# The second feed-forward layer of a Trainium2 decoder step without a plain pair: seven products for its first pair of hidden tiles too, three of them on plain blocks ahead

## The chip, the core and the metric

The kernel runs on one core of a Trainium2 chip. The metric is the device time of one execution in microseconds (us). Five engines work side by side, each through its own queue in order: TensorE multiplies matrices (PE in the rows, PEld for its weight loads), VectorE (DVE) and ScalarE (ACT) work elementwise, GpSimd (POOL) adds squares, and SyncE (SP) issues the DMAs that bring weights from HBM. Semaphores order them.

## The reference

One inference step of a decoder trunk of two layers over 544 tokens (512 of a prompt, 32 of eight samples), model width 1024. Each layer has a half feed-forward, a token mixer (a gMLP in the first layer, attention in the second), a second half feed-forward and a gated embedding. What matters here is the gMLP's end and the feed-forward behind it:

```
def rmsnorm(x, g):
    y = xf * lax.rsqrt(jnp.mean(xf * xf, axis=-1, keepdims=True) + EPS)
    return (y * g.astype(jnp.float32)).astype(x.dtype)
def swiglu(x, w1, w3, w2):
    return (jax.nn.silu(x @ w1) * (x @ w3)) @ w2
...
        h = h + 0.5 * swiglu(rmsnorm(h, ffn1_norm[i]), ffn1_w1[i], ffn1_w3[i], ffn1_w2[i])
        ...
            mix, v_rows = gmlp_mix(xn, gmlp_w_in[i], gmlp_v_norm[i], gmlp_w_s[i], gmlp_b_s[i], gmlp_w_out[i])
        h = h + mix
        h = h + 0.5 * swiglu(rmsnorm(h, ffn2_norm[i]), ffn2_w1[i], ffn2_w3[i], ffn2_w2[i])
```

`w1` and `w3` are 1024 x 2816, so there are 22 hidden tiles of 128, or 11 pairs.

## The kernel before

Everything is held transposed: the residual `h` lies in 8 chunks of 128 model rows by 544 tokens. For accuracy every float32 operand is split into a high and a low half (`_split`, `split_pair`, `prep`): ScalarE casts the high half, VectorE subtracts it for the low one, and each product is three matmuls (high by high, high by low, low by high).

**Two ways to multiply a pair of hidden tiles.** A plain pair is four calls of `tile_mm` (two hidden tiles, `w1` and `w3` of each): 8 blocks of 128 rows, three matmuls, two column groups (256 and 288 tokens), so 48 matmuls each. Every other pair goes by seven products (`ffn_steps.products`, names "1" to "7" as in `SEVEN`): weights are cut in four quarters a11, a12, a21, a22, tokens in two halves of 272, and chunks of `h` in pairs. Product 1 is a11 on the even chunks' first half, 2 is a12 on the odd chunks' first half, 3 is (a12 - sum 6) on the odd chunks' second half; 5, 6, 7 and 4 work on sums of chunk blocks, which `forms` makes for a pair of chunks: two scalings on ScalarE, three subtractions on VectorE, two splits. Weight sums are made by VectorE in `_sum`: 5 = a21 + a22, 6 = sum 5 - a11, 7 = a11 - a21. One product is 4 blocks x 3 x 2 = 24 matmuls of 272 columns; `evict` adds the seven sums up, and `gate` puts the norm's `rstd`, the silu and the product of the two branches behind it.

**What comes before the layer.** The gMLP ends with 8 tiles of `tile_mm(m)`. Behind each, VectorE adds the tile to `h[c]` and `on_chunk` (in `next_norm`) makes the next layer's operand chunk (`prep`), its square on ScalarE and the running sum of squares on GpSimd; `early` names chunks after which the forms of a pair are made at once. Forms 0 to 2 are made there; the fourth is made during the plain pair, by `more` in `ffn`. The row statistic `rstd` goes by four short matmuls on the summed squares (`rstd`), in the first plain tile.

**Order.** Weights stand in one list of pieces; `prepare` loads, sums and splits ahead of use by the three numbers of `self.ahead` (split, sums, load, in pieces). In the gMLP the order of each engine's instructions is made by the framework's scheduler, which works from its own estimate of times; in `ffn_steps` it is the order of the code, with `ffn_slots` listing products and second-matrix pieces. `PLAIN = (2, 1, 1, 1)` gives the plain pairs of the four feed-forwards.

Of the kernel before, what the change touches and what calls it, by code (L numbers as in the profile page):

```python
# [54 lines left out]
PLAIN = (2, 1, 1, 1)  # L55

SEVEN = "1562734"

# [36 lines left out]
class Builder:  # L95
# [37 lines left out]
    def set_stream(self):  # L133
        self.chain, self.pending, self.bg, self.pages = None, [], [], {}
        self.aps, self.raws = [], {}
        self.pieces, self.sums, self.split = [], {}, {}
# [12 lines left out]
    def seven(self, aps):  # L149
# [5 lines left out]
        for k, x, op, y in (("5", a21, "+", a22), ("6", (r, "5"), "-", a11), ("7", a11, "-", a21),  # L155
                            ("3", a12, "-", (r, "6"))):
            d[k] = dict(key=(r, k), sum=(x, op, y))
        for v in d.values():
            v.update(n=1024)
# [14 lines left out]

    def _sum(self):
        p = self.pieces[self.p_sum]
        self.p_sum += 1
        if p["sum"] is None:
            return
        a, op, b = p["sum"]  # L180
        get = lambda x: self._raw(x, 1024) if isinstance(x[1], int) else self.sums[x]
        a, b = get(a), get(b)
        t = self.flat(1024)
        self.nc.vector.tensor_tensor(t, a, b, ALU.add if op == "+" else ALU.subtract)  # L184
        self.sums[p["key"]] = t
# [184 lines left out]
    def ffn_slots(self, skip=1):  # L370
# [16 lines left out]
    def ffn_pieces(self, n):  # L387
# [4 lines left out]
        for kind, at, k, part in self.ffn_slots(PLAIN[n]):  # L392
            if kind == "g":
                if at not in d:
                    d[at] = self.seven([i["w13"][n, at - 1, x] for x in range(4)])
# [10 lines left out]
    def ffn(self, h, box, gcol, rstd, on_chunk, plain=1):  # L406
# [33 lines left out]
        with self.tc.manual_schedule(engines={eng.PE, eng.Activation, eng.DVE, eng.Pool}):  # L440
            self.ffn_steps(h, xf, rstd, hid, todo, plain, on_chunk)
# [23 lines left out]
    def ffn_steps(self, h, xf, rstd, hid, todo, plain, on_chunk):  # L465
# [8 lines left out]
        def products(j, k, part):  # L474
            if k == "1" and j not in tiles:
                tiles[j] = {}
            t = tiles[j]
            if k in "152" and "ABC"["125".index(k)] not in t:
                if k == "2":
                    t["B"] = [self.pb()[:, :HT] for _ in range(2)]  # L480
                else:
                    t["A" if k == "1" else "C"] = self.ps()[:, :, :HT]
            out = t["A" if k in "1674" else "C" if k in "53" else "B"]
            dst = out if k == "2" else [out[:, w] for w in range(2)]
            hi, lo = self.take()
            for kp in range(NKP):
                xh, xl = xf[kp][k]
                for n, (a, b) in enumerate(((hi, xh), (hi, xl), (lo, xh))):
                    for w in range(2):
                        c = slice(512 * w + P * kp, 512 * w + P * kp + P)  # L490
                        nc.tensor.matmul(dst[w], a[:, c], b, start=k in "152" and kp == 0 and n == 0,  # L491
# [3 lines left out]
        def evict(j, k):  # L495
            t = tiles[j]
            if k in "156":
                t["r" + k] = q2(self.tmp())
                nc.scalar.copy(t["r" + k], t["C" if k == "5" else "A"])  # L499
                return  # L500
            if k == "2":
                t["g"] = self.big(), self.big()
            g = t["g"]
# [5 lines left out]
            elif k == "3":  # L509
                tt(g[0][:, :, HT:], t["C"], t["r6"], add)  # L510
                todo[0].extend(self.gate(hid, rstd, j, 0, g[0]))
            else:
# [57 lines left out]
    def gmlp(self, h, box, on_chunk):  # L570
# [94 lines left out]
        for c in range(NC_):  # L665
            p = self.tile_mm(m)
# [631 lines left out]
    def build(self):  # L1298
# [76 lines left out]
        on, nxt = self.next_norm(h, G_FFN2, early={1: 0, 3: 1, 5: 2})  # L1375
# [3 lines left out]
        self.ffn(h, box, G_FFN2, None, on)  # L1379
# [135 lines left out]
```

## Time and profile before

| what | value |
|---|---|
| time, median of 3 runs | 2065.02 us (2064.1 to 2067.02) |
| the profiled execution's own time | 2064.99 us |
| its span, first to last instruction | 2063.2 us |
| TensorE busy | 2043.9 us, 99%, 16432 matmuls |
| VectorE busy | 1507.6 us, 73% |
| ScalarE busy | 949.2 us, 46% |
| GpSimd busy | 186.9 us, 9% |
| granted TensorE clock, mean of the core | 1.000 |

The profile gives times from the span's start. A timeline row has the start, the time from its first instruction's start to its last one's end, engine, source line, operation, what it writes and reads, how many are merged, and in brackets how long the engine was idle before it and who ended that. A recorded duration holds a tail that the next instruction of the engine may overlap.

### The profile page before, as it was taken

How to read it: one execution, taken by the hardware profiler on the slowest of the kernel's cores; microseconds unless marked ns; L12 is line 12 of the kernel's file. 1: busy time of each engine (PE TensorE's matmuls, PEld its weight loads, DVE VectorE, ACT ScalarE, POOL GpSimd, SP SyncE). 2: the span in 40 equal slices, each digit the busy share in tenths (PEclk: the TensorE clock that was granted, in tenths of full speed). 3: DMA queues.
4: the chain of work that ended last, by engine and by line, in shares of the span. 5: the costliest groups of instructions: out<-in, count | busy, mean ns of one | idle time of the engine just before them, and what ended most of it. 6: DMA issues, size and time to landing. Idle time of an engine off the chain costs nothing.

```text
span 2063.2 us, 38844 instructions
## 1 busy us (share of the span) xinstructions
PE 2043.9 (99%) x16432; PEld 2012.0 (98%) x16432; DVE 1507.6 (73%) x1869; ACT 949.2 (46%) x1405; POOL 186.9 (9%) x238
## 2 busy tenths in 40 slices
PE   8999999999999999999999999999999999999999
PEld 8999999999999999999999999999987999999999
DVE  7877777556687777776688777776476888777774
ACT  7534344423554344454456343434364754344451
POOL 0000000410100000043060000001142200000020
PEclk9999999999999999999999999999999999999999
DMA  5233234312223232432374322324669322322431
GB/s 185 84 110 108 73 108 141 97 44 83 83 92 113 73 106 80 153 99 82 109 260 156 112 93 102 108 71 130 201 208 305 103 101 82 104 103 82 128 99 44
DMA packets 93807, 237.95 MB, mean 115 GB/s; under 512 B 9522, under 2 KB 27474, under 8 KB 93634
## 3 DMA queue, kind: packets, MB, share of 16 engines
q1 hardware_dynamic: 93490, 235.44, 34.4%
q8 instruction: 129, 2.11, 0.4%
q14 instruction: 44, 0.36, 0.1%
q10 hardware_dynamic: 144, 0.04, 0.0%
HBM read 218.95 MB, written 16.49 MB: 114 GB/s over the span
## 4 chain that ended last, share of the span: by engine, by line
PE 93%; DVE 3%; ACT 2%; issue 1%; DMA 1%; SPq 0%; POOL 0%; DVEq 0%; ACTq 0%
PE ps L491 33%; PE ps L241 16%; PE ps L247 16%; PE ps L245 16%; PE pb L491 5%; DVE big L199 1%; PE ps L1265 1%; PE ps L1269 1%; PE ps L1268 1%; ACT big L198 1%; PE ps L1222 0%; DVE big L184 0%; PE ps L829 0%; PE ps L830 0%; PE ps L831 0%
## 5 line engine op out<-in xcount | busy, mean ns | idle before, releaser
L491 PE MATMUL ps<-big,big 128*128 128x272 f32 x5616 | 727.7, 288 | 1.8 <-DVE big L508 1.3
L491 PEld LDWEIGHTS ps<-big,big 128*128 128x128 f32 x5616 | 714.2, 188 | 2.4 <-issue 1.6
L199 DVE TENSOR_TENSOR big<-big,big 128x1024 fp32r<-128x1024 f32 (+2 forms) x538 | 592.2, 1103 | 106.6 <-ACT big L198 106.0
L198 ACT CAST big<-big 128x1024 fp32r<-128x1024 f32 (+2 forms) x538 | 488.0, 932 | 267.8 <-DVE big L184 262.8
L241 PE MATMUL ps<-big,big 128*128 128x256 f32 (+1 forms) x2684 | 559.0, 289 | 7.2 <-ACT big L198 7.2
L247 PE MATMUL ps<-big,big 128*128 128x256 f32 x2684 | 554.5, 288 | 1.3 <-DVE big L199 1.3
L245 PE MATMUL ps<-big,big 128*128 128x256 f32 x2684 | 554.0, 287 | 0.0
L241 PEld LDWEIGHTS ps<-big,big 128*128 128x128 f32 x2684 | 430.5, 189 | 10.7 <-ACT big L198 7.4
L245 PEld LDWEIGHTS ps<-big,big 128*128 128x128 f32 x2684 | 432.9, 189 | 0.0
L247 PEld LDWEIGHTS ps<-big,big 128*128 128x128 f32 x2684 | 429.8, 188 | 3.1 <-DVE big L199 2.7
L326 POOL TENSOR_TENSOR st<-st,tmp 128x544 f32<-128x544 f32 (+1 forms) x63 | 87.4, 1387 | 1589.1 <-ACT tmp L324 1589.0
L530 DVE SCALAR_TENSOR_TENSOR big<-ps,big 128x544 f32<-128x544 f32 x160 | 115.6, 723 | 106.5 <-PE ps L247 106.4
L184 DVE TENSOR_TENSOR big<-big,big 128x1024 f32<-128x1024 f32 x156 | 190.1, 1219 | 0.0
L499 ACT COPY tmp<-ps 128x544 f32<-128x544 f32 x117 | 71.7, 613 | 141.3 <-PE ps L491 141.3
L454 ACT ACTIVATE big<-big 128x544 f32<-128x544 f32 x88 | 58.0, 660 | 163.3 <-DVE big L451 162.1
L491 PE MATMUL pb<-big,big 128*128 128x272 f32 x936 | 124.0, 288 | 0.0
L451 DVE TENSOR_TENSOR big<-big,st 128x1088 f32<-128x1088 f32 x88 | 113.7, 1293 | 10.6 <-ACT big L513 8.9
L491 PEld LDWEIGHTS pb<-big,big 128*128 128x128 f32 x936 | 120.2, 188 | 0.0
L297 ACT ACTIVATE big<-big,gains 128x544 fp32r<-128x544 f32 (+1 forms) x80 | 55.8, 704 | 118.4 <-DVE big L530 64.9
L286 DVE TENSOR_TENSOR big<-big,big 128x544 fp32r<-128x544 f32 (+1 forms) x112 | 80.9, 728 | 36.2 <-ACT big L285 36.1
L298 DVE SCALAR_TENSOR_TENSOR big<-big,gains,big 128x544 fp32r<-128x544 f32 (+1 forms) x80 | 66.0, 832 | 26.1 <-ACT big L297 26.1
L285 ACT CAST big<-big 128x544 fp32r<-128x544 f32 (+1 forms) x112 | 71.3, 644 | 16.0 <-DVE big L457 8.9
(208 smaller groups left out, 1435.6 us busy)
## 6 DMA issues: line engine op xcount, KB each, us to landing
big<-in_w SPq DMA_DIRECT2D x156, 512.0 KB
big<-in_w2a SPq DMA_DIRECT2D x64, 512.0 KB
big<-in_w2b SPq DMA_DIRECT2D x32, 384.0 KB
big<-in_w13p SPq DMA_DIRECT2D x16, 512.0 KB
big<-in_win SPq DMA_DIRECT2D x16, 512.0 KB
big<-in_wg SPq DMA_DIRECT2D x16, 512.0 KB
big<-in_ck SPq DMA_DIRECT2D x16, 512.0 KB
big<-in_cv SPq DMA_DIRECT2D x16, 512.0 KB
```

The lines of the kernel that those rows point to most:

```text
L184: self.nc.vector.tensor_tensor(t, a, b, ALU.add if op == "+" else ALU.subtract)
L198: self.nc.scalar.copy(hi, src)
L199: self.nc.vector.tensor_tensor(lo, src, hi.bitcast(F32), ALU.subtract)
L241: i = nc.tensor.matmul(out[:, a:b], wh, xh[:, a:b], start=s, stop=False)
L245: nc.tensor.matmul(out[:, a:b], wh, xl[:, a:b], start=False, stop=False)
L247: nc.tensor.matmul(out[:, a:b], wl, xh[:, a:b], start=False, stop=e)
L286: self.nc.vector.tensor_tensor(pair[:, 1, cols], src, pair[:, 0, cols].bitcast(F32), ALU.subtract)
L326: nc.gpsimd.tensor_tensor(acc[:, cols], acc[:, cols], sq, ALU.add)
L451: tt(g, g, rstd.unsqueeze(1).broadcast_to([P, 2, T]), ALU.mult)
L491: nc.tensor.matmul(dst[w], a[:, c], b, start=k in "152" and kp == 0 and n == 0, stop=kp == NKP - 1 and n == 2, skip_group_check=True)
L499: nc.scalar.copy(t["r" + k], t["C" if k == "5" else "A"])
L530: nc.vector.scalar_tensor_tensor(h[c], whole(out), 0.5, h[c], ALU.mult, ALU.add)
```

## The change

The second feed-forward (number 1 in `PLAIN`) has no plain pair: its pair 0 goes by seven products. Their order is `PLAIN_FIRST`: 1, 2 and 3 first, which use chunk blocks and no forms; then the row statistic (now called in `products` before 6), then 6, 5 and 7; product 4 of pair 0 stands behind the first product of pair 1. Product 3, which comes ahead of 6 here, has sums of its own (D). The fourth forms are made in the gMLP's last `on_chunk` (`7: 3` in `early`). From the gMLP's output tile 5 on `self.ahead` is (2, 3, 6). A weight sum is made when it is asked for, with those that it needs (`_operand`). The stacked weights `w13` hold all 11 pairs.

```
-PLAIN = (2, 1, 1, 1)
+PLAIN = (2, 0, 1, 1)
+PLAIN_FIRST = "123657"
...
+    def _operand(self, x):
+        if isinstance(x[1], int):
+            return self._raw(x, 1024)
+        if x not in self.sums:
+            a, op, b = self.defs[x]
+            a, b = self._operand(a), self._operand(b)
+            t = self.flat(1024)
+            self.nc.vector.tensor_tensor(t, a, b, ALU.add if op == "+" else ALU.subtract)
+            self.sums[x] = t
+        return self.sums[x]
...
-            gs = [("g", j, k, None) for k in SEVEN]
+            gs = [("g", j, k, None) for k in (SEVEN if j else PLAIN_FIRST)]
+            if j == 1 and skip == 0:
+                gs.insert(1, ("g", 0, "4", None))
...
         def products(j, k, part):
+            nonlocal rstd
+            if rstd is None and k == "6":
+                rstd = self.rstd(acc)
...
-            if k in "152" and "ABC"["125".index(k)] not in t:
+            own = "3" if j == 0 else ""
+            fresh = k in "152" + own
+            if fresh:
...
-            if k in "156":
+            if k in "15" or k == ("6" if j else "3"):
                 t["r" + k] = q2(self.tmp())
-                nc.scalar.copy(t["r" + k], t["C" if k == "5" else "A"])
-                return
+                nc.scalar.copy(t["r" + k], t["C" if k == "5" else "D" if k == "3" else "A"])
+            if j == 0 and k == "6":
+                tt(t["r3"], t["A"], t["r3"], add)
...
-            elif k == "3":
-                tt(g[0][:, :, HT:], t["C"], t["r6"], add)
+            elif k == ("3" if j else "5"):
+                tt(g[0][:, :, HT:], t["C"], t["r6" if j else "r3"], add)
...
         for c in range(NC_):
+            if c == NC_ - 3:
+                self.ahead = (2, 3, 6)
             p = self.tile_mm(m)
...
-        on, nxt = self.next_norm(h, G_FFN2, early={1: 0, 3: 1, 5: 2})
+        on, nxt = self.next_norm(h, G_FFN2, early={1: 0, 3: 1, 5: 2, 7: 3})
...
-        self.ffn(h, box, G_FFN2, None, on)
+        self.ffn(h, box, G_FFN2, None, on, PLAIN[1])
```

The order of the instructions changes in two places. The first is VectorE's queue behind the gMLP's last tile. In both pieces big6_89 is the residual's chunks 6 and 7. Before, from the split of the last output weights on (lines of the kernel before; big727 is chunk 7's operand, whose low half L298 makes):

```order
L199 TENSOR_TENSOR big724_5929<-big708_5794,big723_5928 128x1024
L667 TENSOR_TENSOR big6_89<-ps726_5934,big6_89 128x544
L298 SCALAR_TENSOR_TENSOR big727_5984<-big6_89,gains_84,big727_5984 128x544
L199 TENSOR_TENSOR big731_5992<-big719_5870,big730_5991 128x1024
L358 TENSOR_TENSOR tmp735_6041<-st671_5510,tmp734_6040 128x544
L199 TENSOR_TENSOR big741_6062<-big725_5932,big740_6061 128x1024
```

Now (lines of the changed kernel; big723 is a12, big725 its low half, big726, big727 and big728 are the sums 5, 6 and 3, big730 is chunk 7's operand, tmp733 and tmp734 the steps of the fourth forms, big735 and big736 their splits, big739 the low half of 3's weights):

```order
L687 TENSOR_TENSOR big6_89<-ps729_5940,big6_89 128x544
L208 TENSOR_TENSOR big725_5931<-big723_5928,big724_5930 128x1024
L186 TENSOR_TENSOR big726_5934<-big718_5868,big719_5870 128x1024
L186 TENSOR_TENSOR big727_5936<-big726_5934,big702_5732 128x1024
L186 TENSOR_TENSOR big728_5938<-big723_5928,big727_5936 128x1024
L307 SCALAR_TENSOR_TENSOR big730_5990<-big6_89,gains_84,big730_5990 128x544
L320 TENSOR_TENSOR tmp733_5999<-big732_5996 128x544
L322 TENSOR_TENSOR tmp734_6000<-big732_5996,tmp733_5999 128x272
L323 TENSOR_TENSOR tmp734_6000<-big732_5996,tmp734_6000 128x272
L295 TENSOR_TENSOR big735_6001<-tmp733_5999,big735_6001 128x544
L295 TENSOR_TENSOR big736_6002<-tmp734_6000,big736_6002 128x544
L208 TENSOR_TENSOR big739_6038<-big728_5938,big738_6037 128x1024
```

Between the tile's addition and chunk 7's low half (L298, now L307) stand one split and three sums that did not stand there, and the fourth forms come right behind it.

The same place on ScalarE. Before, from chunk 7's high half (L297) to the statistic's cast (L357, of the summed squares st671):

```order
L297 ACTIVATE big727_5984<-big6_89,gains_84 128x544
L324 ACTIVATE tmp728_5987<-big6_89 128x544
L198 CAST big730_5991<-big719_5870 128x1024
L357 CAST tmp734_6040<-st671_5510 128x544
L426 COPY big729_5990<-ps733_5997 128x544
```

Now, from the casts of the fourth forms on (big738, big740, big745 and big754 are the high halves of the weights of 3, 6, 5 and 7):

```order
L294 CAST big735_6001<-tmp733_5999 128x544
L294 CAST big736_6002<-tmp734_6000 128x544
L207 CAST big738_6037<-big728_5938 128x1024
L207 CAST big740_6041<-big727_5936 128x1024
L516 COPY tmp744_6071<-ps737_6012 128x544
L207 CAST big745_6073<-big726_5934 128x1024
L207 CAST big754_6114<-big747_6077 128x1024
L366 CAST tmp756_6118<-st671_5510 128x544
```

The statistic's cast stands third behind chunk 7's high half before, and now behind the forms' casts and four weight casts. VectorE's half of it stands behind the same weights' low halves.

The second place is in the attention, among VectorE's score reductions. Before (ps2034 and ps2035 hold scores, the sm tiles one column each):

```order
L1123 TENSOR_REDUCE sm2039_16952<-ps2034_16922 128x1
L1123 TENSOR_REDUCE sm2042_16959<-ps2035_16923 128x1
L1125 RECIPROCAL sm2040_16953<-sm2040_16953 128x1
L1125 RECIPROCAL sm2043_16960<-sm2043_16960 128x1
L1123 TENSOR_REDUCE sm2045_16966<-ps2035_16923 128x1
```

Now (ps2048 and ps2049 are the same tiles):

```order
L1143 TENSOR_REDUCE sm2053_16957<-ps2048_16927 128x1
L1145 RECIPROCAL sm2054_16958<-sm2054_16958 128x1
L1143 TENSOR_REDUCE sm2056_16964<-ps2049_16928 128x1
L1145 RECIPROCAL sm2057_16965<-sm2057_16965 128x1
L1143 TENSOR_REDUCE sm2059_16971<-ps2049_16928 128x1
```

The second of two reductions that stood together has moved behind a reciprocal.

## Rows read from the trace of the kernel before

**Rows 1.** The page: busy time by engine; the chain that ended last.
```profile
PE 2043.9 (99%) x16432; PEld 2012.0 (98%) x16432; DVE 1507.6 (73%) x1869; ACT 949.2 (46%) x1405; POOL 186.9 (9%) x238
...
PE 93%; DVE 3%; ACT 2%; issue 1%; DMA 1%; SPq 0%; POOL 0%; DVEq 0%; ACTq 0%
```

**Rows 2.** Windows: the plain pair of the second feed-forward, with its column line.
```profile
core 0: us, PE busy (x) PEld busy (x) DVE busy (x) ACT busy (x) POOL busy (x), PEclk, DMA share, GB/s
540.00:564.40 24.40, 24.40 (x199) 24.40 (x198) 13.37 (x17) 10.36 (x15) 1.36 (x1) 1.00 0.16 50
```

**Rows 3.** Timeline of TensorE, from the plain pair on.
```profile
540.10 0.41 PE L241 MATMUL ps<-big,big 128*128 128x256 f32 x2
...
564.50 9.23 PE L491 MATMUL ps<-big,big 128*128 128x272 f32 x72
573.56 3.19 PE L491 MATMUL pb<-big,big 128*128 128x272 f32 x24
...
583.50 8.75 PE L491 MATMUL ps<-big,big 128*128 128x272 f32 x68 [0.72 <-DVE big L508]
```

**Rows 4.** Timeline of VectorE behind the gMLP's last tile.
```profile
540.30 0.72 DVE L667 TENSOR_TENSOR big<-ps,big 128x544 f32<-128x544 f32 x1 [0.54 <-PE ps L247]
541.90 0.79 DVE L298 SCALAR_TENSOR_TENSOR big<-big,gains,big 128x544 fp32r<-128x544 f32 x1 [0.88 <-ACT big L297]
543.39 1.62 DVE L199 TENSOR_TENSOR big<-big,big 128x1024 fp32r<-128x1024 f32 x1 [0.70 <-ACT big L198]
```

**Rows 5.** Timeline of ScalarE behind the gMLP's last tile.
```profile
541.12 0.75 ACT L297 ACTIVATE big<-big,gains 128x544 fp32r<-128x544 f32 x1 [3.73 <-DVE big L667]
541.77 0.64 ACT L324 ACTIVATE tmp<-big 128x544 f32<-128x544 f32 x1
542.32 1.03 ACT L198 CAST big<-big 128x1024 fp32r<-128x1024 f32 x1
543.96 0.65 ACT L357 CAST tmp<-st 128x544 fp32r<-128x544 f32 x1 [0.60 <-POOL st L326]
```

**Rows 6.** Timeline of GpSimd: the last square added.
```profile
542.56 1.36 POOL L326 TENSOR_TENSOR st<-st,tmp 128x544 f32<-128x544 f32 x1 [4.52 <-ACT tmp L324]
```

**Rows 7.** Timeline of VectorE: a sum, the fourth forms, product 2's additions.
```profile
561.52 1.22 DVE L184 TENSOR_TENSOR big<-big,big 128x1024 f32<-128x1024 f32 x1
562.65 0.72 DVE L311 TENSOR_TENSOR tmp<-big 128x544 f32<-128x544 f32 x1
563.41 0.44 DVE L313 TENSOR_TENSOR tmp<-big,tmp 128x272 f32<-128x272 f32 x1
...
564.24 0.72 DVE L286 TENSOR_TENSOR big<-tmp,big 128x544 fp32r<-128x544 f32 x1
...
579.67 0.78 DVE L506 TENSOR_TENSOR big<-pb,tmp 128x272 f32<-128x272 f32 x2
```

**Rows 8.** Timeline of ScalarE: the fourth forms' scalings and cast, a copy from the sums.
```profile
560.24 1.39 ACT L307 ACTIVATE big<-big,gains 128x544 f32<-128x544 f32 x2
563.41 0.65 ACT L285 CAST big<-tmp 128x544 fp32r<-128x544 f32 x1 [1.78 <-DVE tmp L311]
...
567.71 0.61 ACT L499 COPY tmp<-ps 128x544 f32<-128x544 f32 x1
```

**Rows 9.** Timeline of SyncE: the plain pair's four loads.
```profile
492.33 24.40 SPq L165 DMA_DIRECT2D big<-in_w13p  x4
```

**Rows 10.** Timeline of TensorE at the start of the program.
```profile
6.94 0.82 PE L241 MATMUL ps<-big,big 128*128 128x256 f32 x2 [6.94 <-ACT big L198]
...
11.54 0.66 PE L241 MATMUL ps<-big,big 128*128 128x256 f32 x2
12.00 0.66 PE L245 MATMUL ps<-big,big 128*128 128x256 f32 x2
...
13.33 0.41 PE L245 MATMUL ps<-big,big 128*128 128x256 f32 x2
```

**Rows 11.** Timeline of VectorE in the attention: score reductions.
```profile
1505.35 0.87 DVE L1123 TENSOR_REDUCE sm<-ps 128x1 f32<-128x256 f32 x2
1506.38 0.16 DVE L1125 RECIPROCAL sm<-sm 128x1 f32<-128x1 f32 x1 [0.17 <-ACT tmp L1124]
```

More of the change, by code (lines that the diff above doesn't have):

```diff
@@ L135, in set_stream @@
         self.aps, self.raws = [], {}
-        self.pieces, self.sums, self.split = [], {}, {}
+        self.pieces, self.sums, self.split, self.defs = [], {}, {}, {}
         self.p_next = self.p_split = self.p_sum = self.a_load = 0
@@ L157, in seven @@
             d[k] = dict(key=(r, k), sum=(x, op, y))
+            self.defs[r, k] = x, op, y
         for v in d.values():
@@ L177, in _sum @@
         self.p_sum += 1
-        if p["sum"] is None:
-            return
[L180 to L185, printed above, removed]
+        if p["sum"]:
+            self._operand(p["key"])
     def _split(self):
@@ L394, in ffn_pieces @@
                 if at not in d:
-                    d[at] = self.seven([i["w13"][n, at - 1, x] for x in range(4)])
+                    d[at] = self.seven([i["w13"][n, at, x] for x in range(4)])
                 self.pieces.append(d[at][k])
@@ L440, in ffn @@
         with self.tc.manual_schedule(engines={eng.PE, eng.Activation, eng.DVE, eng.Pool}):
-            self.ffn_steps(h, xf, rstd, hid, todo, plain, on_chunk)
+            self.ffn_steps(h, xf, rstd, hid, todo, plain, on_chunk, box.get("acc"))
         self.ahead = (2, 2, 4)
@@ L463, in gate, with ffn_steps @@
         return [one, two, three, four]
-    def ffn_steps(self, h, xf, rstd, hid, todo, plain, on_chunk):
+    def ffn_steps(self, h, xf, rstd, hid, todo, plain, on_chunk, acc):
         nc = self.nc
@@ L481, in products @@
                 else:
-                    t["A" if k == "1" else "C"] = self.ps()[:, :, :HT]
-            out = t["A" if k in "1674" else "C" if k in "53" else "B"]
+                    t["A" if k == "1" else "C" if k == "5" else "D"] = self.ps()[:, :, :HT]
+            out = t["A" if k in "1674" else "D" if k in own else "C" if k in "53" else "B"]
             dst = out if k == "2" else [out[:, w] for w in range(2)]
@@ L490, in products @@
                         c = slice(512 * w + P * kp, 512 * w + P * kp + P)
-                        nc.tensor.matmul(dst[w], a[:, c], b, start=k in "152" and kp == 0 and n == 0,
+                        nc.tensor.matmul(dst[w], a[:, c], b, start=fresh and kp == 0 and n == 0,
                                          stop=kp == NKP - 1 and n == 2, skip_group_check=True)
@@ L508, in evict @@
                 tt(g[1][:, :, HT:], t["A"], t["r5"], add)
-            elif k == "3":
-                tt(g[0][:, :, HT:], t["C"], t["r6"], add)
+            elif k == ("3" if j else "5"):
+                tt(g[0][:, :, HT:], t["C"], t["r6" if j else "r3"], add)
                 todo[0].extend(self.gate(hid, rstd, j, 0, g[0]))
-            else:
+            elif k == "4":
                 nc.scalar.copy(g[1][:, :, :HT], t["A"])
@@ L1450, in _arrays @@
         w13p.append(np.stack([_stationary(w1[n][:, :256]), _stationary(w3[n][:, :256])]))
-        w13.append(np.stack([_blocks(w1[n][:, 256:]), _blocks(w3[n][:, 256:])], 3).reshape(NPAIR - 1, 4, P, 1024))
+        w13.append(np.stack([_blocks(w1[n]), _blocks(w3[n])], 3).reshape(NPAIR, 4, P, 1024))
         s = _stationary(w2[n])
```

3 lines of the change are left out of this document (1 added, 2 removed).

## The prediction

> **What bounds the kernel now.** I read the page first: TensorE is busy 99% of a span of 2063.2 us, and the chain that ended last is 93% TensorE and 3% VectorE [rows 1]. So every matmul left out is time won, but only where TensorE does not wait instead. Next I took the table of windows for the stretch that the change rewrites, 540.00 to 564.40, from behind the gMLP's last tile to the end of the plain pair: TensorE is busy for all 24.40 us at a granted clock of 1.00, which is 2.4 GHz, while VectorE works 13.37 us and ScalarE 10.36 us [rows 2]. Then I read the timelines engine by engine: the plain pair runs without a gap from 540.10 to 564.50, and the only wait nearby is 0.72 us at 583.50 [rows 3]; VectorE is never late in the plain pair, since between tile 7's addition at 540.30 and TensorE there stands one short step, the low half of chunk 7 at 541.90 [rows 4]. What I then ask is how long each queue is, as the change orders it, between that addition and each operand that TensorE needs.
>
> **What it removes.** Four plain tiles of 48 matmuls (192) become seven products of 24 (168); four matmuls for the row statistic stay. The 196 took 24.40 us, or 0.1245 us each [rows 3]. The 72 matmuls of three products took 573.56 - 564.50 = 9.06 us, or 0.126 us each, 3.02 us a product [rows 3], so 172 take 21.64 us. Gain: 24.40 - 21.64 = 2.76 us. I also take away the 0.72 us at 583.50 (a product waiting for VectorE to empty its sums): the same place is counted anew below. DMA: four loads of 512 KB replace four, in the same place of SyncE's queue; those were issued from 492.33 to 516.73 [rows 9], 24 us ahead of first use, so I cost them at nothing. Were that cover gone, VectorE's sums would start later and every wait below would grow by the delay.
>
> **What it adds to VectorE's queue.** The first piece of the order shows it: behind tile 7's addition stand the low half of a12, three sums (5, 6 and 3, each needing the one before), and only then the low half of chunk 7, then the four steps of the fourth forms with their two low halves, and only then the low halves of 3, 6 and 5. In the old order the low half of chunk 7 came right behind the addition. The sums stand there because `self.ahead` of (2, 3, 6) from tile 5 on lets `prepare` make the third product's sum with tile 7, and `_operand` makes 5 and 6 on the way. TensorE's second product needs chunk 7 at its nineteenth matmul; its third product needs the weights of 3.
>
> I walk along the queues with durations from the rows. A following instruction begins 0.08 us before the recorded end of the one ahead, one that needs its result 0.04 us after it (562.65 + 0.72, then 563.41) [rows 7], and one that waits for another engine likewise (ScalarE's cast ends at 543.35, VectorE begins at 543.39) [rows 4, 5]. A 1024-wide subtraction or sum takes 1.22 us, a 1024-wide cast 1.03, a 544-wide subtraction 0.72, half of it 0.44, a 544-wide cast 0.65, the two scalings of a form 1.39, a copy from the sums 0.61, the two additions of product 2 0.78 [rows 5, 7, 8].
>
> The addition of tile 7 stays at 540.30, since no instruction ahead of it slows TensorE. ScalarE: square 541.12 to 541.76, high half of a12 541.67 to 542.70, high half of chunk 7 to 543.36, scalings to 544.65. GpSimd adds the square from 541.91 to 543.27, by the 1.36 us of its row and the 0.15 us between them before [rows 5, 6]. VectorE: low half of a12 from 542.75. In the kernel before, the same subtraction took 1.62 us at 543.39 while GpSimd's addition still ran to 543.92 [rows 4, 6]; the new one meets it the same way, so I take 1.62 again: 544.37. Bounds: 1.22 and 1.62, a difference of 0.40 for everything behind it. The Trainium skill (SBUF — State Buffer, "Who interferes with whom") says that a VectorE instruction with two SBUF inputs and a reading GpSimd instruction lock each other out, whoever begins first. By that rule 0.40 is due here; without it the sum below is 0.40 less. This trace's 1.62 against 1.22 bears the rule out.
>
> On: the three sums end at 545.51, 546.77 and 548.03, the low half of chunk 7 at 548.74, the forms' steps at 549.38, 549.86 and 550.34, their low halves at 550.98 and 551.81. ScalarE casts sum 3 from 550.95 to 551.98 (behind the forms' casts), so its low half ends at 553.26, that of 6 at 554.40, that of 5 at 555.68; sum 7 at 556.82; product 2's additions at 557.52; 7's halves at 557.91 and 559.18. The statistic is queued behind all of these on both engines (second piece of the order): high half of the squares' sum 558.47, low half 559.81. In the kernel before it was cast at 543.96, two microseconds behind chunk 7 [rows 5].
>
> TensorE: product 1 from 540.10 to 543.12. Product 2: four matmuls, then a wait for a12's low half until 544.41 (0.79 us); sixteen more to 546.43, then a wait for chunk 7's low half until 548.78 (2.35); four more to 549.28. Product 3: a wait for its high half until 552.03 (2.75), four matmuls, a wait for its low half until 553.30 (0.77), twenty more to 555.82. Statistic: waits until 558.51 (2.69) and, after two matmuls, until 559.85 (1.09); it ends at 560.10. These six waits are 10.44 us. VectorE is then behind by its whole queue. Product 7 adds onto the sums of 1 and 6, which VectorE must read first, seven instructions after the statistic (one split, four steps of the reciprocal root with the wait for ScalarE ahead of them, then the read): about 566.7 against 566.15 on TensorE, a wait of 0.6. Product 4, now put behind the next pair's first, must wait until VectorE has read the sums of 7 (two 1024-wide sums, two splits and three more), about 573.95 against 572.80: 1.15. Both are estimates from the same durations; below they end at 0, above at 2.5 us, twice the greater plus a little. I take 1.75, since they are of the kind of the 0.72 at 583.50. Waits in all: 12.19 us.
>
> **A second place.** In the attention the scheduler puts the third score reduction behind a reciprocal that waits for ScalarE (third piece of the order). In the trace the two reductions run together at 1505.35 and the reciprocal begins at 1506.38 [rows 11]; the third reduction thus moves from about 1505.7 to 1506.46, 0.75 us later, and ScalarE's exponentials and TensorE's next scores hang on it. I take 0.7; bounds 0 and 0.8.
>
> **Sum.** -2.76 - 0.72 + 12.19 + 0.7 = +9.41 us on the profiled execution's 2064.99 us, which agrees with the median of 2065.02: 2074.4 us, 0.46% slower. What this kernel can tell from no change is about 0.2%, 4.1 us.
>
> **Rivals.**
> *The three products cover it* (the other side). TensorE's 9.06 us of plain blocks outlast one pass of the forms: in the kernel before, the steps of the fourth forms took from the scalings at 560.24 to the first low half's end at 564.96, 4.7 us [rows 7, 8]. Without waits the sum is -2.76 - 0.72 = -3.48, so 2061.5 us. It decides if chunk 7's low half is there by 546.4 and that of 3 by 549.6; the three sums would have to stand ahead of the addition, where VectorE had only 0.54 us of idle time [rows 4]. The order says the contrary. Chance 0.05.
>
> *The statistic hides.* If casts of its squares came earlier than I read, 2.69 + 1.09 fall out, and what is behind moves up: 9.41 - 3.78 = 5.6, so 2070.6 us. For it: the squares are summed by 543.3. Against it: in-order queues. Chance 0.08.
>
> *The clock falls too.* At the start TensorE idled 6.94 us and then stepped 12.00 - 11.54 = 0.46 us per two matmuls (the 1.2 GHz level) until 13.33 [rows 10], against 0.249 in the plain pair. Those 6.4 us would have taken 3.5 at the full clock, so a fall costs up to 2.9 us: 2077.3. Between 546.4 and 553.3 TensorE would have 8 matmuls to do, which no stretch of the kernel before comes near after its start; against it, a slower product 3 ends before its successors' operands come, so most of the loss lies beside waits already counted. The Trainium skill (TensorE: Matmul & The Clock Gate, "HAM oscillation — how this bites in real kernels") says that idle gaps between bursts send the array back to half its clock; that speaks for this rival, and no row here shows it behind the start. Chance 0.07.
>
> **How the numbers follow.** The forecast itself, waits at the places named, gets 0.80; its own range, by the bounds of 0.40, 0 to 2.5 and 0 to 0.8, is 2071.5 to 2075.3, and since each of some thirty durations may be off by a few hundredths, 2070 to 2077. To hold the time 8 times in 10 I reach to the neighbours: 2069.0 to 2077.6. Slower by over 0.2%: the forecast, the clock and most of the hidden statistic, less a little for a queue misread: 0.90. Within 0.2%: the cover rival and partial waits, 0.07. Faster: 0.03.
>
> **What would show it.** In the changed profile's timeline of TensorE: a first wait inside product 2, then one ahead of product 3 of two to three microseconds, and one ahead of the statistic, some 12 us of idle between 540 and 575, and the next pair's start about 8 us late; VectorE's three sums back to back from about 544.3, chunk 7's low half near 548. It is wrong if TensorE runs through the three plain products without a gap, if the sums come before the addition, or if the granted clock leaves 1.00 and matmuls step 0.46 us per two.

## The result, and the profile after

The changed kernel takes 2074.84 us (median of 6 runs, 2073.97 to 2075.54) beside 2065.53 us for the kernel before (6 runs, 2064.1 to 2067.02). The ratio is 1.0046, with a 95% interval of 1.0037 to 1.0056: it is slower, by 9.3 us. The forecast was 2074.4 us. The profiled execution after took 2074.97 us with a span of 2073.2 us, 10.0 us more than before.

The page after, busy time by engine and the chain that ended last (to compare with [rows 1]):

```profile
PE 2044.5 (99%) x16408; PEld 2010.8 (97%) x16408; DVE 1519.3 (73%) x1881; ACT 952.1 (46%) x1408; POOL 185.0 (9%) x238
...
PE 90%; DVE 4%; ACT 2%; DMA 2%; issue 1%; SPq 1%; POOL 0%; DVEq 0%; ACTq 0%
```

TensorE has 24 matmuls fewer and is yet busy 0.6 us longer; VectorE has 12 instructions and 11.7 us more. The share of 99% says nothing about the 10 us that were lost. The windows behind the gMLP's last tile do (columns as in [rows 2]: busy time and instructions of TensorE, its weight loads, VectorE, ScalarE and GpSimd, then the granted clock):

```profile
540.00:545.00 5.00, 4.34 (x35) 4.13 (x34) 3.28 (x3) 3.53 (x5) 1.37 (x1) 1.00 0.60 220
545.00:550.00 5.00, 2.04 (x15) 1.60 (x13) 4.86 (x8) 0.68 (x2) 0.00 (x0) 1.00 0.19 76
550.00:555.00 5.00, 3.40 (x13) 3.09 (x14) 4.61 (x5) 3.96 (x5) 0.00 (x0) 0.50 0.10 38
555.00:560.00 5.00, 3.55 (x20) 3.12 (x19) 3.91 (x6) 1.78 (x3) 0.00 (x0) 0.81 0.00 0
560.00:565.00 5.00, 5.00 (x42) 5.00 (x41) 2.77 (x5) 3.08 (x5) 0.00 (x0) 1.00 0.18 37
```

Before, TensorE was busy through all of this [rows 2]. Now it is busy for 2.04 of the 5 us from 545 on, while VectorE is busy for 4.86, and right behind that the granted clock is 0.50, the 1.2 GHz level. Its timeline tells which operand it waited for (start, length, line, merged instructions, idle time before and releaser):

```profile
539.66 3.18 PE L508 MATMUL ps<-big,big 128*128 128x272 f32 x24
542.67 0.67 PE L508 MATMUL pb<-big,big 128*128 128x272 f32 x4
543.99 2.28 PE L508 MATMUL pb<-big,big 128*128 128x272 f32 x16 [0.66 <-DVE big L208]
548.34 0.77 PE L508 MATMUL pb<-big,big 128*128 128x272 f32 x4 [2.06 <-DVE big L307]
551.61 5.81 PE L508 MATMUL ps<-big,big 128*128 128x272 f32 x24 [2.50 <-ACT big L207]
558.03 0.51 PE L371 MATMUL pb<-tmp,onesr 128*128 128x272 f32 x2 [0.61 <-ACT tmp L366]
559.38 0.52 PE L371 MATMUL pb<-tmp,onesr 128*128 128x272 f32 x2 [0.84 <-DVE tmp L367]
559.74 6.20 PE L508 MATMUL ps<-big,big 128*128 128x272 f32 x48
566.30 6.27 PE L508 MATMUL ps<-big,big 128*128 128x272 f32 x48 [0.36 <-DVE tmp L518]
573.52 9.26 PE L508 MATMUL ps<-big,big 128*128 128x272 f32 x72 [0.96 <-DVE big L526]
582.62 3.16 PE L508 MATMUL pb<-big,big 128*128 128x272 f32 x24
```

Products 1, 2 (in pieces of 4, 16 and 4) and 3, the statistic (L371), products 6 and 5, then 7 with the next pair's first, then 4 and two more. Product 3 has 24 matmuls like product 1 and takes 5.81 us instead of 3.18: the half clock. VectorE at the same place, to compare with [rows 4]:

```profile
539.86 0.72 DVE L687 TENSOR_TENSOR big<-ps,big 128x544 f32<-128x544 f32 x1 [1.68 <-PE ps L256]
542.31 1.63 DVE L208 TENSOR_TENSOR big<-big,big 128x1024 fp32r<-128x1024 f32 x1 [1.72 <-ACT big L207]
543.86 3.73 DVE L186 TENSOR_TENSOR big<-big,big 128x1024 f32<-128x1024 f32 x3
547.51 0.78 DVE L307 SCALAR_TENSOR_TENSOR big<-big,gains,big 128x544 fp32r<-128x544 f32 x1
...
558.61 0.72 DVE L367 TENSOR_TENSOR tmp<-st,tmp 128x544 fp32r<-128x544 f32 x1
```

The three sums stand back to back (x3 at 543.86) ahead of chunk 7's low half at 547.51, which began at 541.90 before [rows 4]; the statistic's low half, the last row, begins at 558.61, where its high half had been cast at 543.96 before [rows 5].

Two more stretches, in the attention. The third reduction now follows a reciprocal (VectorE, compare [rows 11]), and TensorE's scores behind it wait 1.26 us, where the same wait was 0.48 us before. Later a small DMA of `rows` lands late, and VectorE waits 0.71 us for it:

```profile
1513.82 0.41 DVE L1143 TENSOR_REDUCE sm<-ps 128x1 f32<-128x256 f32 x1
1514.86 0.16 DVE L1145 RECIPROCAL sm<-sm 128x1 f32<-128x1 f32 x1 [0.63 <-ACT tmp L1144]
1514.93 0.54 DVE L1143 TENSOR_REDUCE sm<-ps 128x1 f32<-128x384 f32 x1
...
1540.39 0.79 DVE L1077 SCALAR_TENSOR_TENSOR big<-big,gains,tmp 128x544 f32<-128x544 f32 x1 [0.71 <-DMA tmp<-rows]
```

TensorE's two waits there, first in the kernel before:

```profile
1508.57 0.44 PE L1105 MATMUL ps<-big,big 128*128 128x384 f32 x1 [0.48 <-ACT tmp L1124]
...
1532.95 2.44 PE L1184 MATMUL pb<-big,big 128*32 128x128 f32 x80 [0.17 <-POOL big L1171]
```

And in the changed kernel:

```profile
1517.83 0.45 PE L1125 MATMUL ps<-big,big 128*128 128x384 f32 x1 [1.26 <-ACT tmp L1144]
...
1542.97 2.44 PE L1204 MATMUL pb<-big,big 128*32 128x128 f32 x80 [0.82 <-POOL big L1191]
```

The second of them, 0.82 us, was 0.17 us in the profile before; GpSimd's copy (L1191), which TensorE waits for, needs what VectorE makes from those `rows`.

### The profile page after: what moved, and what is told of

Same layout as the page of the kernel before. It is cut to its first block, busy times and chain, and to the rows that moved or that the text cites. A ratio compares the mean times of both kernels' runs of the same rounds, so it can differ in the third digit from the quotient of the medians.

```text
span 2073.2 us, 38816 instructions
## 1 busy us (share of the span) xinstructions
PE 2044.5 (99%) x16408; PEld 2010.8 (97%) x16408; DVE 1519.3 (73%) x1881; ACT 952.1 (46%) x1408; POOL 185.0 (9%) x238
## 3 DMA queue, kind: packets, MB, share of 16 engines
q8 instruction: 129, 2.11, 0.4%
## 4 chain that ended last, share of the span: by engine, by line
PE 90%; DVE 4%; ACT 2%; DMA 2%; issue 1%; SPq 1%; POOL 0%; DVEq 0%; ACTq 0%
PE ps L508 33%; PE ps L250 15%; PE ps L256 15%; PE ps L254 15%; PE pb L508 6%; DVE big L208 1%; DMA tmp<-rows 1%; ACT big L207 1%; PE ps L1285 1%; PE ps L1289 1%; PE ps L1288 1%; DVE big L186 1%; PE ps L1242 0%; DVE big L295 0%; PE ps L849 0%
## 5 line engine op out<-in xcount | busy, mean ns | idle before, releaser
L508 PE MATMUL ps<-big,big 128*128 128x272 f32 x5760 | 749.0, 289 | 4.8 <-ACT big L207 2.5
L250 PE MATMUL ps<-big,big 128*128 128x256 f32 (+1 forms) x2620 | 545.0, 289 | 7.4 <-ACT big L207 7.4
L256 PE MATMUL ps<-big,big 128*128 128x256 f32 (+1 forms) x2620 | 541.2, 288 | 1.8 <-DVE big L208 1.8
L254 PE MATMUL ps<-big,big 128*128 128x256 f32 (+1 forms) x2620 | 540.3, 287 | 0.0
L186 DVE TENSOR_TENSOR big<-big,big 128x1024 f32<-128x1024 f32 x160 | 195.1, 1219 | 0.1
L307 DVE SCALAR_TENSOR_TENSOR big<-big,gains,big 128x544 fp32r<-128x544 f32 (+1 forms) x80 | 65.9, 832 | 24.8 <-ACT big L306 24.7
```

The source lines that it names most:

```text
L250: i = nc.tensor.matmul(out[:, a:b], wh, xh[:, a:b], start=s, stop=False)
L254: nc.tensor.matmul(out[:, a:b], wh, xl[:, a:b], start=False, stop=False)
L256: nc.tensor.matmul(out[:, a:b], wl, xh[:, a:b], start=False, stop=e)
L508: nc.tensor.matmul(dst[w], a[:, c], b, start=fresh and kp == 0 and n == 0, stop=kp == NKP - 1 and n == 2, skip_group_check=True)
```

## The experiments

My theory: VectorE's in-order queue, from tile 7's addition to the operands of products 2 and 3, the statistic and what follows, is longer than the matmuls that cover it. The rivals: the order of that queue alone decides; the statistic's place decides; the fall of the clock decides. Each edit is against the changed kernel unless another is named, and kernel 2 is the kernel of experiment 2. Each ratio is to the kernel before, run again beside the experiment (medians of 2064.90 to 2065.48 us).

**1. The plain pair kept, everything else of the change left in.**

```
-PLAIN = (2, 0, 1, 1)
+PLAIN = (2, 1, 1, 1)
```

> The changed kernel with the plain pair put back in the second feed-forward (PLAIN of 1): the fourth forms still behind the gMLP's last tile, the longer look-ahead kept. Theory (VectorE's queue between tile 7's addition and the operands of products 2 and 3 is longer than the two products that cover it): 24 us of plain tiles cover it, so no wait appears, and the 0.72 us at 583.50 goes too, since the fourth forms are out of the way there: about 0.9 us below the kernel before, 2064.6 us. Rival (the early forms and the look-ahead cost by themselves, whatever TensorE does meanwhile): 2068 us or more.

Measured: 2064.38 us, ratio 0.9995 (0.9986 to 1.0004). The window over the plain pair:

```profile
540.00:564.00 24.00, 24.00 (x195) 24.00 (x195) 14.50 (x19) 11.53 (x17) 1.37 (x1) 1.00 0.21 67
```

TensorE has no gap and keeps its clock. The code around the pair (sums made on demand, the new look-ahead) costs nothing by itself: the loss comes with the seven products, as the change orders them.

**2. The sums earlier: with tiles 5 and 6 instead of behind tile 7.**

```
-                self.ahead = (2, 3, 6)
+                self.ahead = (2, 5, 6)
```

> The changed kernel with a look-ahead for sums of 5 pieces in place of 3: the three sums stand one tile earlier, behind the gMLP's tile 5, nothing else. Theory: the queue behind tile 7's addition is 3.7 us shorter; the wait for chunk 7's low half (2.1 us) goes and the one ahead of product 3 falls from 2.5 us to about 1.0; the waits for the statistic stay. Walked with the same durations: 4.5 us less than the changed kernel, plus 0.7 less in the attention, whose old order is back: 2069.3 us. Rival (VectorE has too much work in the whole stretch, wherever it stands): the waits move into the gMLP's tiles, 2074 to 2075 us.

Measured: 2070.06 us, ratio 1.0023 (1.0014 to 1.0033), 4.8 us less than the change. TensorE's timeline, from product 2 on:

```profile
542.52 3.19 PE L508 MATMUL pb<-big,big 128*128 128x272 f32 x24
547.39 0.77 PE L508 MATMUL ps<-big,big 128*128 128x272 f32 x4 [1.68 <-ACT big L207]
548.65 4.12 PE L508 MATMUL ps<-big,big 128*128 128x272 f32 x20 [0.49 <-DVE big L208]
553.81 0.52 PE L371 MATMUL pb<-tmp,onesr 128*128 128x272 f32 x2 [1.04 <-ACT tmp L366]
...
555.78 13.46 PE L508 MATMUL ps<-big,big 128*128 128x272 f32 x96
```

Product 2 runs without a wait, and product 3 starts 7.88 us behind product 1 (539.51) instead of 11.95. The layer as a whole is 3.9 us shorter, and 0.8 us of the 4.8 come from the attention, where the old order is back (table below). Moving three sums of VectorE (3.73 us) takes about their own time out of the waits, as a queue that is too long demands. The clock falls here too (0.66 granted from 555 to 560), and it lies open: the 96 matmuls behind the statistic take 13.46 us, where they would take about 12.2 at the full clock. The time is 0.8 us above the expected 2069.3.

**3. The old look-ahead: the three sums behind the forms' steps and partly among them.**

```
-            if c == NC_ - 3:
-                self.ahead = (2, 3, 6)
```

> The changed kernel without the longer look-ahead: chunk 7's low half stands right behind tile 7's addition again, and the three sums come behind the fourth forms. Theory (the length of the queue up to product 3's weights decides, not its order): the two waits in product 2 go, and the wait ahead of product 3 grows from 2.5 us to about 5.2; with the attention's old order 2073.5 us. Rival (the place of the sums ahead of chunk 7's low half decides, as the prediction's wording has it): the waits in product 2 go and none grows, 2070.7 to 2071.5 us.

Measured: 2073.01 us, ratio 1.0038 (1.0025 to 1.0052). TensorE:

```profile
542.75 3.19 PE L508 MATMUL pb<-big,big 128*128 128x272 f32 x24
551.08 5.18 PE L508 MATMUL ps<-big,big 128*128 128x272 f32 x24 [5.14 <-ACT big L207]
557.50 0.52 PE L371 MATMUL pb<-tmp,onesr 128*128 128x272 f32 x2 [1.24 <-ACT tmp L366]
```

The waits in product 2 are gone, and one wait of 5.14 us ahead of product 3 has taken their place: product 3 starts 11.35 us behind product 1 (539.73), the changed kernel's 11.95. The rival by which the order alone decides falls; the work between the addition and the operand counts, and its order only says where TensorE stands still. By the median this kernel is 1.8 us ahead of the change, by the two profiled runs 2.0 us: 0.6 us of these come from this layer, 0.8 us from the attention, whose old order is back, and 0.7 us from the wait for the `rows` behind it, which changes from profile to profile (table below).

**4. The statistic late: its matmuls ahead of product 7, its halves cast before product 3's weights.**

```
+            if acc is not None and rstd is None and k == "3":
+                halves.extend(self.rstd_parts(acc))
-            if rstd is None and k == "6":
-                rstd = self.rstd(acc)
+            if rstd is None and k == "7":
+                rstd = self.rstd(acc, halves)
+                self.advance()
```

> The changed kernel with the row statistic's matmuls ahead of product 7 in place of product 6, and its casts one step earlier: TensorE does not wait for it behind product 3. In the changed kernel's trace the granted clock fell to half in 550 to 556 us, and product 3 took 5.81 us, yet it cost nothing visible, since the statistic was waited for anyway. Theory A (the clock's fall was hidden by that wait and is a cost of its own): with the wait gone the slow product 3 is laid open, some 2.3 us of the 3.9 that the wait was worth are lost, so 2072.5 us. Theory B (the slow clock is no cost): 3.9 us and the attention's 0.7 less than the changed kernel, 2070.2 us.

Measured: 2073.89 us (2071.36 to 2074.56), ratio 1.0043 (1.0029 to 1.0057): no measurable gain in the median. The profiled run is the fastest of the five, 3.6 us below the changed kernel's profiled run, so its rows show where the time goes in that run and not in the median:

```profile
551.09 12.12 PE L516 MATMUL ps<-big,big 128*128 128x272 f32 x72 [2.50 <-ACT big L207]
563.04 0.66 PE L376 MATMUL pb<-tmp,onesr 128*128 128x272 f32 x4
563.54 6.18 PE L516 MATMUL ps<-big,big 128*128 128x272 f32 x48
571.83 9.26 PE L516 MATMUL ps<-big,big 128*128 128x272 f32 x72 [2.11 <-DVE big L534]
```

Both waits of the statistic are gone. But three products in one piece take 12.12 us, where 9.23 us is the full clock's time [rows 3], so the half clock now costs what the wait had hidden, as theory A has it; and product 4 waits 2.11 us instead of 0.96 for VectorE. A part of this second wait may be the edit's own, since VectorE stands idle for 1.31 us before 564.51, waiting for the later statistic; in experiment 5 that idle time is absent and the wait is 2.12 us all the same. In this profile the layer is 1.2 us shorter than the changed kernel's, not 3.9. By the median both expectations missed: a wait that is taken out of a chain of waits comes back, in part at least, at the next one. Why the five runs differ by 3 us isn't settled. The three runs of 2073.89 to 2074.56 us have a mean granted clock of 0.997 and the two near 2071.6 us one of 0.998, which would fit a longer fall in the slower ones, but only one of the five has a profile.

**5. The same, with 20 matmuls on product 1's operands put ahead of product 3** (they write into its sums and are overwritten; the wait stays busy).

```
+            if j == 0 and k == "3":
+                for n in range(20):
+                    nc.tensor.matmul(out[:, n % 2], fill[0][:, :P], xf[0]["1"][0], start=True, stop=True,
+                                     skip_group_check=True)
```

> As the run before (statistic ahead of product 7), and 20 matmuls on old operands are put ahead of product 3, into sums that product 3 then starts anew; they stand in TensorE's wait for its weights (2.5 us) and change no result. Theory A (clock): TensorE is not idle, product 3 runs at the full clock in about 3.8 us with its wait for the low half, and the time is 2 us below the run before: 2070.3 us. Theory B (clock is no matter): the same time as the run before.

Measured: 2073.13 us (2070.84 to 2073.71), ratio 1.0037 (1.0023 to 1.005). In its profile the three products run at the full clock (68 matmuls in 8.78 us from 552.98), and the fall comes later, behind the next wait:

```profile
570.40 10.81 PE L522 MATMUL ps<-big,big 128*128 128x272 f32 x72 [2.12 <-DVE big L540]
```

72 matmuls in 10.81 us, with a granted clock of 0.66 from 570 to 575. Theory A's 2070.3 us, which had no fall at all in it, missed by the median. Theory B's "the same time" came true as far as the scatter of both kernels lets one tell, but not for its reason: the fall has moved to product 4 and costs again.

**6. The 20 matmuls alone, in the changed kernel** (the edit of 5 without that of 4).

> The changed kernel with the same 20 filling matmuls ahead of product 3 and nothing else. If the clock's fall was hidden by the wait for the statistic, product 3 is faster by 2 us, the wait for the statistic longer by as much, and the time the changed kernel's, 2074.5 to 2075 us. If the slow clock cost something after all, 2072 to 2073 us.

Measured: 2075.85 us, ratio 1.0053 (1.0039 to 1.0067). TensorE:

```profile
538.99 3.18 PE L514 MATMUL ps<-big,big 128*128 128x272 f32 x24
...
552.21 2.77 PE L514 MATMUL ps<-big,big 128*128 128x272 f32 x20 [0.49 <-DVE big L208]
557.37 0.82 PE L371 MATMUL pb<-tmp,onesr 128*128 128x272 f32 x2 [2.39 <-ACT tmp L366]
558.72 0.82 PE L371 MATMUL pb<-tmp,onesr 128*128 128x272 f32 x2 [0.53 <-DVE tmp L367]
559.34 23.54 PE L514 MATMUL ps<-big,big 128*128 128x272 f32 x168
```

At the full clock product 3 is over by 555, and the statistic waits 2.39 us, near the 2.69 us that the prediction had; nothing is won. Its matmuls begin 18.38 us behind product 1's start here and 18.37 us in the changed kernel (558.03 less 539.66). So up to there the changed kernel's slow product 3 cost nothing: it lay where TensorE would have waited. Here the half clock moved to the products behind the statistic, where it is not covered (granted clock 0.69 from 555 to 560 and 0.63 from 560 to 565): the layer is 0.8 us longer than the changed kernel's, and the time is above both expected ranges.

**7. Everything early: sums and one more split ahead, the statistic's halves before product 1's weights, its matmuls ahead of product 7, product 4 two places later** (with the edit of 4, "3" read as "1").

```
-                gs.insert(1, ("g", 0, "4", None))
+                gs.insert(3, ("g", 0, "4", None))
-                self.ahead = (2, 3, 6)
+                self.ahead = (3, 5, 6)
```

> The changed kernel with all that the theory names moved out of the way: sums 5, 6 and 3 with tile 6 and product 3's and 2's splits one piece earlier (look-ahead 3, 5, 6), the squares' casts ahead of product 1, the statistic ahead of product 7, and product 4 of pair 0 behind two more products of pair 1. Theory: waits of 0.3, 1.8, 0.2 and 0.4 us are left, less than the 3.5 us that the matmuls and the old wait are worth: 2064.6 us, 0.9 below the kernel before, too little to be told from it. Rival (seven products on this pair cost VectorE more than the matmuls save, wherever it is put): 2067 us or more.

Measured: 2065.86 us, ratio 1.0003 (0.9994 to 1.0012). One wait is left, and a half clock behind it:

```profile
544.26 0.77 PE L516 MATMUL ps<-big,big 128*128 128x272 f32 x4 [1.79 <-DVE big L307]
544.87 4.70 PE L516 MATMUL pb<-big,big 128*128 128x272 f32 x24
```

What TensorE waited for, and what GpSimd did at that time:

```profile
542.31 1.90 DVE L307 SCALAR_TENSOR_TENSOR big<-big,gains,big 128x544 fp32r<-128x544 f32 x1
...
542.29 1.33 POOL L335 TENSOR_TENSOR st<-st,tmp 128x544 f32<-128x544 f32 x1 [2.26 <-ACT tmp L333]
```

Nine of the 9.3 us are back with the same seven products (0.8 us of them in the attention, where the old order stands again). What made the change slow is where the helpers' work stands, VectorE's above all, and not the products. The edit moves several things at once; only the sums (experiment 2) and the statistic (4) were tried apart. The wait left is inside product 1: chunk 6's low half now stands behind the split of a12 in VectorE's queue, and it takes 1.90 us beside GpSimd's addition, where chunk 7's takes 0.77. So, as an estimate, some 1.1 of the 1.79 us come from the two engines' meeting and not from the queue's order; GpSimd's addition was moved in no experiment. The expected waits had that 1.8 us, but not the fall of the clock behind it (product 2 in 4.70 us instead of 3.19), so the time is 1.3 us above the expected 2064.6; the rival's 2067 us missed too.

**8 and 9. The look-ahead two tiles sooner**, both against kernel 7; the edit shown is that of 8, and 9 has (4, 6, 7) instead.

```
-            if c == NC_ - 3:
-                self.ahead = (3, 5, 6)
+            if c == NC_ - 5:
+                self.ahead = (3, 6, 7)
```

> As the kernel with all early, but from output tile 3 on the three numbers are (3, 6, 7). So the three sums and the split of a12 are made two tiles sooner, and chunk 6's low half stands ahead of tile 7's addition in VectorE's queue. Theory (VectorE's queue behind tile 7 is all that made the change slow): TensorE waits under 0.3 us anywhere between 536 and 560, the clock stays at 1.00, and what is left is 24 matmuls fewer and no wait of 0.72 at 583.50: -2.76 - 0.72 + 0.6 for small waits that remain = about -2.9, so 2062.0 us beside 2064.9 to 2065.5, a ratio of 0.9986. Rival (the sums, wherever they stand, delay VectorE by as much, here tile 7's addition by about 1.1 us, and some operand is late all the same, with the clock falling behind it as before): one wait of 1 to 2 us inside product 1 or ahead of product 3 and a stretch at half clock, 2065 to 2066 us.

> The same with (4, 6, 7) from output tile 3 on: one more weight piece is split ahead, so that tile 7's addition is not delayed, but the low half of a12 stands between it and chunk 6's low half again, as in the kernel with all early, where TensorE waited 1.79 us inside product 1. Theory (queue order): a wait inside product 1 of 1 to 2 us, with half clock behind it, and none at products 2 and 3: 2064.5 to 2066 us. Rival (that wait came from the sums and not from the place of chunk 6's low half): no wait, 2062 us.

Measured: 2064.57 us, ratio 0.9997 (0.9988 to 1.0006), and 2063.70 us, ratio 0.9993 (0.9984 to 1.0002). Kernel 8, TensorE behind product 1:

```profile
543.14 3.19 PE L516 MATMUL pb<-big,big 128*128 128x272 f32 x24
546.16 3.17 PE L516 MATMUL ps<-big,big 128*128 128x272 f32 x24
550.60 6.57 PE L516 MATMUL ps<-big,big 128*128 128x272 f32 x48 [1.25 <-ACT tmp L524]
```

The three plain products now run without a gap, and product 6 waits 1.25 us for ScalarE to copy product 1's sums, a copy that stands behind the forms' casts and a weight cast. Both expectations missed: the clock stayed at 1.00 as the theory had it, but with this wait, and with the attention's new order, which the theory had not counted, the time is 2.6 us above the expected 2062.0. Kernel 9, TensorE:

```profile
544.01 0.77 PE L516 MATMUL ps<-big,big 128*128 128x272 f32 x4 [1.52 <-DVE big L307]
544.62 3.16 PE L516 MATMUL pb<-big,big 128*128 128x272 f32 x24
```

The wait for chunk 6's low half is there as expected, at 1.52 us, but the clock stayed at 1.00, so the time came out below the expected 2064.5. As in kernel 7, the low half that it waits for met GpSimd's addition and took 1.87 us. Of the 2.76 + 0.72 us that the seven products can save, 0.8 us are left in kernel 8 and 1.7 us in kernel 9, against the 2065.37 us of the kernel before beside them; neither is measurably faster than the kernel before, since both intervals reach past 1. In kernel 9 VectorE is busy 5.00 of the 5 us from 540 and 4.93 of the next 5: the stretch is full.

**The layer and what lies behind it, in one profile each.** The layer is the time from product 1's start (the plain pair's, before) to the start of product 2 of the next pair, in TensorE's rows; the two waits are TensorE's in the attention and behind it, as in the last fences of the section above. These three belong to the profiled run, whose own time stands beside the median.

| kernel | layer, us | attention wait | wait behind it | profiled run, us | median, us |
|---|---|---|---|---|---|
| before | 33.46 | 0.48 | 0.17 | 2064.99 | 2065.53 |
| changed | 42.96 | 1.26 | 0.82 | 2074.97 | 2074.84 |
| 2 | 39.08 | 0.48 | 0.75 | 2069.82 | 2070.06 |
| 3 | 42.34 | 0.48 | 0.16 | 2072.95 | 2073.01 |
| 4 | 41.79 | 0.49 | 0.49 | 2071.36 | 2073.89 |
| 5 | 41.29 | 0.49 | 1.58 | 2073.20 | 2073.13 |
| 6 | 43.73 | 1.28 | 1.71 | 2075.85 | 2075.85 |
| 7 | 34.43 | 0.50 | 0.64 | 2066.02 | 2065.86 |
| 8 | 32.71 | 1.28 | 1.12 | 2065.11 | 2064.57 |
| 9 | 32.73 | 0.49 | 0.82 | 2063.74 | 2063.70 |

Kernels 8 and 9 have equal layers; 8 has the attention's new order and 9 the old one, which is 0.8 us in the attention's wait; the medians differ by 0.87 us. The last wait lies anywhere between 0.16 and 1.71 us, and I see no relation to the edits.

## Why the prediction was right

**What it removes** came out as worked out. The 24 matmuls are gone, and the wait of 0.72 us at 583.50 [rows 3] has no successor: 144 matmuls follow each other without a gap from 585.62.

**VectorE's queue** was right nearly to the row. TensorE reached product 1 at 539.66, 0.44 us earlier than before, so 0.44 is added here to compare: the sums began at 544.30 (544.3 forecast), chunk 7's low half at 547.95 (547.95, its end at 548.74 less 0.79). VectorE met GpSimd as counted: a12's low half took 1.63 us at 542.31 while GpSimd added from 541.48 to 542.85, and the 0.40 us taken from the rows for it were right. The lock that the Trainium skill states (SBUF — State Buffer, "Who interferes with whom") agrees with this trace once more.

**The waits**, each worked out as the start of a row less the start of the one ahead and 0.126 us for each of its matmuls:

| place | forecast, us | measured, us |
|---|---|---|
| product 2, a12's low half | 0.79 | 0.82 |
| product 2, chunk 7's low half | 2.35 | 2.33 |
| product 3, high half of its weights | 2.75 | 2.77 |
| product 3's start to the statistic's | 6.48 | 6.42 |
| statistic, its second half | 1.09 | 1.10 |
| product 7 | 0.6 | 0.51 |
| product 4 | 1.15 | 1.17 |

From product 1's start to product 4's it comes to 33.86 us; the forecast's 573.95 - 540.10 was 33.85. Two of the signs that the prediction named did not come as worded. TensorE's recorded idle time from 540 to 575 is 8.0 us (27.02 us busy of 35), not some 12, since product 3's slowness fills most of the wait for the statistic. And the next pair's product 1 starts at 569.3 (24 matmuls behind 566.30), 4.8 us later than at 564.50 [rows 3] and not 8; the forecast's own walk gives about 5.

**The clock**, a rival with a chance of 0.07, was wrong in the forecast as an event and right as a time. The clock did fall, to 0.50 for 550 to 555, and by the prediction's own last sentence that is a sign of its being wrong. The forecast's fourth row of 6.48 us was 0.77 of wait, 3.02 of product 3 and 2.69 of wait for the statistic; what happened was 5.81 us of a product at 1.2 GHz and 0.61 us of recorded wait. The sum is the same, since the statistic's cast on ScalarE set the end in both. Experiment 6 shows that: with product 3 at the full clock the statistic waits 2.39 us and begins as late as in the changed kernel. So the fall's price in time was none where I gave it up to 2.9 us, though I had named the reason ("most of the loss lies beside waits already counted"). That it was hidden whole is partly luck: product 3 lost 2.8 us, and 0.61 us of wait was left over; in kernels 2, 4 and 6 a fall in the same layer lies open. The 0.46 us steps at the start, from which the price was taken [rows 10], stand in windows with a granted clock of 1.00, so the granted clock doesn't show that they were the lower level; the size came out alike. The rule of the Trainium skill (TensorE: Matmul & The Clock Gate, "HAM oscillation — how this bites in real kernels"), that gaps between bursts throw the array back to half its clock, is borne out by the window of 0.50 behind 2.04 busy microseconds of five; kernel 9, with a gap of 1.52 us and a clock of 1.00, shows that not every gap does it. What a fall does to the time depends on what lies beside it.

**The attention** was forecast at 0.7 us and measured 1.26 - 0.48 = 0.78.

**What was not in the sum.** The layer came to 42.96 - 33.46 - 0.72 = +8.78 us (forecast 8.71). With the attention's 0.78, the wait behind it (0.82 - 0.17 = 0.65), a start 0.44 us earlier and some 0.2 us spread over many rows, that is the 10.0 us between the two spans. The 0.65 is a DMA that landed late in this profile; experiments 3 and 5 show the same wait at 0.16 and at 1.58 us, so I don't count it to the change, and the medians differ by 9.3 us and not by 10.0. The 0.44 us are no more than what such profiles differ by: kernels 4, 5 and 6, whose edits all stand behind product 1, start it at 539.14, 539.76 and 538.99. With parts of that size left out, a forecast within 0.5 us of the median is closer than the method warrants.

**The other rivals.** Three products don't cover the work as the change orders it, but kernel 8 shows that they can: there all three run in one piece. "The statistic hides" missed by experiment 4: even where its matmuls wait for nothing, the half clock lies open and a later product waits.

## What to carry to other kernels

Before work is taken from the engine that bounds a stretch, add up, instruction by instruction, what stands in the in-order queue of the helping engine between the last event that it must wait for and the first operand that is needed: here 24 matmuls (2.76 us) were saved in the one place where VectorE had no slack, and 12 us of lost time came back. In a chain of such waits, one that is removed reappears at the next operand until the queue itself is shorter or starts earlier (experiments 4 and 5 against 2, 7 and 8). A fall of the clock beside a wait that is counted already cost nothing (the changed kernel); the same fall beside full work did (kernels 2, 4, 5, 6 and 7).

## What the runs showed of the hardware that was not expected

- The granted clock fell without a long pause: from 545 to 550 the changed kernel's TensorE was busy 2.04 us in two bursts, and the clock was 0.50 from 550 to 555. Twenty matmuls more from 548.28 to 550.95 (experiment 6) kept it at 1.00 there, and it fell behind the next wait instead. Experiments 7 and 9 have nearly the same single wait (1.79 and 1.52 us); the clock fell behind the first alone.
- What VectorE loses beside GpSimd's addition of squares goes with what is left of that addition when VectorE's instruction begins. A 128x544 low half (L307, in the kernel before L298) took 1.87 to 1.90 us instead of 0.77 to 0.79 with 1.28 to 1.31 us left (chunk 6's in the kernel before and in kernels 7 and 9, chunk 7's in kernel 2); the 128x1024 low half of the prediction's 0.40 us had 0.53 to 0.54 us left. In each case the loss is 0.13 to 0.20 us less than what was left. Kernel 8 puts chunk 6's low half where GpSimd is at rest, at 540.15, and it takes 0.77 us.
- Behind the attention's late small DMAs (`rows`) TensorE waits anything from 0.16 to 1.71 us in profiles of kernels that share that code, so single profiles can differ by 1.5 us for this alone.
